# Four projection chunks of the HGRN2 mixer as two seven-product pairs, and re-spaced scans

## The chip, the core and the metric

The kernel runs on one NeuronCore of a Trainium2 chip. The metric is the device time of one execution in microseconds. PE is TensorE's matmul part, PEld its weight loads, DVE is VectorE, ACT ScalarE, POOL GpSimd and SP SyncE, which here only issues DMAs.

## The reference, cut to what matters

Two blocks of tokens (512 and 256, together T = 768, width D = 1024, float32) go through two layers. Each layer is half an FFN, a token mixer, and half an FFN; layer 0's mixer is a bidirectional gated linear recurrence (HGRN2), layer 1's is windowed attention. What matters here is the HGRN2 mixer:

```python
def hgrn2_mixer(x, w_in, w_o, g_norm, lb):
    """x: [B,T,D]; w_in: [D,5D] -> q | i | g | f_fwd | f_bwd; lb: [2, H*K] per-direction lower bounds."""
    q, i, g, f_fw, f_bw = jnp.split(x @ w_in, 5, axis=-1)
...
        f = lbd + (1.0 - lbd) * jax.nn.sigmoid(fpre.astype(F32))
        logf = jnp.log(f).reshape(B, T, H, K)
        k = (1.0 - f).reshape(B, T, H, K).astype(x.dtype)
...
    o_fwd = gla_chunk_scan(q, k_f, i, logf_f)
    o_bwd = rev(gla_chunk_scan(rev(q), rev(k_b), rev(i), rev(logf_b)))
    o = (o_fwd + o_bwd).astype(F32)
    o = o * lax.rsqrt(jnp.mean(o * o, axis=-1, keepdims=True) + NORM_EPS)
    o = o * g_norm.astype(F32).reshape(H, V)
    o = o.reshape(B, T, H * V).astype(x.dtype) * jax.nn.silu(g)
    return o @ w_o
```

`gla_chunk_scan` is the recurrence S_t = diag(f_t) S_{t-1} + k_t v_t^T, o_t = S_t^T q_t. There are 8 heads of 128 columns. Each head needs three chunks of the projection, 128 columns each: q (number 0), forward gate (3) and backward gate (4). Values (i) and output gate (g) are projected for all heads together.

## The kernel before, in words

**Float32 from three matmuls.** Each operand is split into a rounded high part (ACT, a cast) and a low remainder (DVE, a subtraction); a product is high x high + high x low + low x high, three matmuls (`mm3`, L312). Weights are loaded raw by SP into the pool "wr" (4 buffers), split into the pool "w" (8 buffers), and used. `plan` and `plan_quad` queue the weights, `ahead` and `take` stage as many as "w" holds, and `stage_next` (L272) loads further raw weights as buffers come free.

**Seven products for eight.** The FFN's up projections, the value, gate and output projections use a Strassen-like scheme: a 2 x 2 block product (two halves of the contraction by two halves of tokens or columns) is made from seven products in place of eight. The token side needs the blocks b00, b01, b10, b11 and the mixed factors t1 to t4, which `mix` (L420) and `put` (L410) make on DVE and ACT; each of the eight occupies two tiles of the pool "big" (21 buffers of 6 KB a partition). `up_pair` (L523) makes a gate and an up column block of the FFN so: seven `product` calls (L508) of 12 matmuls, 384 columns wide. The weight side of a pair (`quad_steps`, L181) takes two raw tiles, one more tile "s" of 256 KB, two accumulating DMAs on POOL's queue (`into`, L146), seven splits and two additions.

**The mixer's order.** `hgrn` (L971) traces, in this order:
1. the lead chunks, `LEAD` = q, forward and backward gate of head 0 and q of head 1, plainly by `hgrn_chunk` (L781): first all four for the first half of the tokens, then all four for the second. With the first half run the deferred steps of the FFN before (transposes, mixed factors, the spill of x);
2. the spill of the mixed factors (POOL's queue, `spill_factors`, L444);
3. the values, `tok_quad` (L742): seven products, 512 columns wide, order p1 p2 p7 p6 p5 p4 p3. Their raw weights (`tok_steps`, L228) take all four "wr" tiles, eight of eight scratch tiles "tA", two "s" and one "big". Inside them come the masks and head 0's gate arithmetic (`hgrn_gates`, L804);
4. one scan per head (`hgrn_scan`, L825). It has seven levels (L851 to L885). A level repacks the keys (L853, ACT), makes the scores of six blocks (L823, PE), evacuates them (`put`, L833: L837 or L842, DVE), multiplies the queries (L875), the keys (L879) and the totals (L881) on DVE. After the levels come transposes of the keys (L896), the states (L904, with a chain of ACT and DVE, L912 and L915) and the outputs (L928).

The scans' chains leave TensorE waiting, so `weave` (L711) puts filler between them: after each of the eight steps of a scan it takes pieces of a stream. The stream is the 20 plain chunks that remain (each six pieces of 9, 9 and 6 matmuls for either half) and then the gate projection (42 pieces). Before, a scan takes 16 pieces (head 0), 18 (heads 1 to 6) or 20 (head 7), evenly spread; what is left of the gate projection comes after.

The framework that builds the program orders each engine's instructions ahead of time, by when their inputs and buffers come free, so an instruction may stand far ahead of its place in the source.

Of the kernel before, what the change touches and what calls it, by code (L numbers as in the profile page):

```python
# [12 lines left out]
AF = mybir.ActivationFunctionType  # L13
# [20 lines left out]
SEQS = ((0, TA), (TA, TB))  # L34
H = T // 2
# [8 lines left out]
UP = ("p1", "p7", "p2", "p5", "p4", "p6", "p3")  # L44
TOK = ("p1", "p2", "p7", "p6", "p5", "p4", "p3")
TCHAIN = {"p2": "p1", "p4": "p5", "p3": "p7"}
OUT = ("p1", "p2", "p3", "p7", "p6", "p4", "p5")
LEAD = ((0, 0), (0, 3), (0, 4), (1, 0))
DOWN = ("p1", "p2", "p5", "p4", "p7", "p6", "p3")
FACTOR = {"p1": "b00", "p2": "b10", "p3": "b11", "p4": "t4", "p5": "t1", "p6": "t2", "p7": "t3"}  # L50


class Trunk:
# [356 lines left out]
    def put(self, name, kp, src, ops=None):  # L410
        if ops is None:
            ops = self.ops
        t = ops[(name, kp)] = self.big([P, 2, 2, H], F32R)
        self.split(src, t[:, :, 0, :], t[:, :, 1, :])
# [293 lines left out]
            yield  # L708

    @staticmethod  # L710
    def weave(main, feed, pieces, steps=LEVELS + 1, also=None):  # L711
        used = 0
        for i, _ in enumerate(main):
            if also:
                also(i)
            while used * steps < (i + 1) * pieces:
                used += 1
                next(feed, None)

    @staticmethod  # L720
# [21 lines left out]
    def tok_quad(self, key, order, chains, ops, evac, seed=None):  # L742
# [35 lines left out]
        for k in used:  # L778
            self.done(k)

    def hgrn_chunk(self, h, hd, c0, halves):  # L781
        key = ("hgrn", h, c0)
        wh, wl = self.take(key)
        if c0 == 0:
            if "qk" not in hd:
                hd["qk"] = self.big([P, 2, T])
            dst, func = hd["qk"][:, 0, :], AF.Copy
        else:
            if "f" not in hd:
                hd["f"] = self.big([P, 2, T])  # L790
            dst, func = hd["f"][:, 4 - c0, :], AF.Sigmoid
        for half in halves:
            ps = self.ps(H)
            for kk in range(NC):
                b = self.operand(f"b{kk // 4}{half}", kk % 4)
                self.mm3(ps, (wh[:, kk, :], wl[:, kk, :]), b, kk == 0, kk == NC - 1)
                if kk in (2, 5):
                    yield
            self.nc.scalar.activation(dst[:, half * H : (half + 1) * H], ps, func)
            if half:  # L800
                self.done(key)
            yield

    def hgrn_gates(self, h, hd):  # L804
        nc = self.nc
        qs, kd, f = hd["qk"][:, 0, :], hd["qk"][:, 1, :], hd["f"]
        q, k = (self.big([P, 2, T]) for _ in range(2))
        for d in range(2):
            fd, j = f[:, 1 - d, :], slice(h, h + 1)
            nc.vector.tensor_scalar(fd, fd, self.om_lb[:, d, j], self.lb[:, d, j], ALU.mult, ALU.add)  # L810
            nc.scalar.activation(k[:, d, :], fd, AF.Identity, bias=1.0, scale=-1.0)
            nc.vector.tensor_mul(q[:, 1 - d, :], qs, fd)
        nc.vector.tensor_add(kd, k[:, 0, :], k[:, 1, :])
        hd.update(h=h, qs=qs, kd=kd, q=q, k=k)

# [9 lines left out]
    def hgrn_scan(self, hd, v):  # L825
        nc = self.nc
        h, qs, kd, f, q, k = (hd[n] for n in ("h", "qs", "kd", "f", "q", "k"))
# [3 lines left out]
        blk = lambda t, b: t[:, b * P : (b + 1) * P]  # L831

        def put(level, pss):  # L833
            for s, (off, n) in enumerate(SEQS):
                dst = A[:, off : off + n]
                if level == 0:
                    nc.vector.tensor_copy(dst, pss[s])  # L837
                    continue
                nb = n // P
                m = self.masks[:, level, :].unsqueeze(1).to_broadcast([P, nb, P])  # L840
                r = lambda t: t.rearrange("p (b j) -> p b j", b=nb)
                nc.vector.copy_predicated(r(dst), m, r(pss[s]))  # L842
# [7 lines left out]
        tot, base = f, 0  # L850
        for l in range(LEVELS):  # L851
            c, J = T >> l, 1 << l
            nc.scalar.copy(packed(kop, J), picked(k, J))  # L853
# [12 lines left out]
            self.scan_scores(pss, lambda b: blk(kop, b), rhs)  # L866
            put(l, pss)
            if l == 0:
                pss = [self.ps(n) for _, n in SEQS]
                self.scan_scores(pss, lambda b: blk(kd, b), lambda b: blk(qs, b))  # L870
                put(LEVELS, pss)
            part = [list(q.ap[0])]
            both = bass.AP(q.tensor, q.offset, part + [[T + J, 2], [2 * J, c // 2], [1, J]])
            t = bass.AP(tot.tensor, tot.offset + base + 1, [list(tot.ap[0]), [T - 1, 2], [2, c // 2], [0, J]])
            nc.vector.tensor_mul(both, both, t)  # L875
            for d in range(2):
                xv = self.halves(k, l, d, d)
                t = tot[:, 1 - d, base + 1 - d : base + c : 2].unsqueeze(2).to_broadcast([P, c // 2, J])
                nc.vector.tensor_mul(xv, xv, t)  # L879
            nbase = 0 if l == 0 else base + c  # L880
            nc.vector.tensor_mul(  # L881
                totals[:, :, nbase : nbase + c // 2], tot[:, :, base : base + c : 2], tot[:, :, base + 1 : base + c : 2]
            )
            tot, base = totals, nbase
            yield  # L885

# [50 lines left out]
            )  # L937

    def plan_hgrn(self, w_in, w_o):
        def chunk(h, c):  # L940
            lo = c * D + h * P
            self.plan(("hgrn", h, c), w_in[:, lo : lo + P], (NC, P))

        for h, c in LEAD:
            chunk(h, c)
        def quad(key, w, order):
            rows = w.rearrange("(k m a p) c -> k m p a c", k=2, m=2, p=P)
            srcs = [[rows[k][m][:, :, c * 512 : (c + 1) * 512] for m in range(2)] for c in range(2) for k in range(2)]
            self.plan_quad(key, srcs, None, order)

        quad(("v",), w_in[:, D : 2 * D], TOK)
        for h in range(1, HEADS):
            for c in (0, 3, 4):
                if (h, c) not in LEAD:
                    chunk(h, c)
        quad(("g",), w_in[:, 2 * D : 3 * D], TOK)
        quad(("o",), w_o, OUT)

# [12 lines left out]
    def hgrn(self, lb_row, gn_row, next_row):  # L971
        nc = self.nc
# [5 lines left out]
        for half in range(2):  # L978
            for n, (h, c) in enumerate(LEAD):
                for i, _ in enumerate(self.hgrn_chunk(h, heads[h], c, (half,))):  # L980
                    if half == 0 and n and i != 1:
                        self.run_later()
            self.run_later(len(self.deferred))
        vs = {}

        def vtile(b):
# [22 lines left out]
        for at in self.tok_quad(("v",), TOK, TCHAIN, self.ops, evac_v):  # L1009
            if at == ("p6", HB - 1, 1):  # L1010
                self.load_masks()
                self.hgrn_gates(0, heads[0])
        scan = lambda hd: self.hgrn_scan(hd, vs)

        def stream():
            for h in range(1, HEADS):
                for c in (0, 3, 4):
                    if (h, c) not in LEAD:
                        yield from self.hgrn_chunk(h, heads[h], c, range(2))
                self.hgrn_gates(h, heads[h])  # L1020

        rs = self.cp.tile([P, HEADS, NBLK], F32, name="hrs")

# [78 lines left out]

        feed = itertools.chain(stream(), gate())
        for h in range(HEADS - 1):
            early = (lambda i, h=h: i in (1, 4) and len(ready) and scaled(*ready.pop(0))) if h > 3 else None
            self.weave(scan(heads[h]), feed, 16 if h == 0 else 18, also=early)
            if h == 3:
                rstds(0, 4)
                ready = [(i, i + 1) for i in range(4)]
        rstds(4, HEADS - 1)  # L1110
        self.weave(scan(heads[-1]), feed, 20, also=lambda i: i in (1, 3, 5) and scaled(4 + i // 2, 5 + i // 2))
        rstds(HEADS - 1, HEADS)
        scaled(HEADS - 1, HEADS)
        for i in range(HB):
# [445 lines left out]
```

## Time and profile before

| | us |
|---|---|
| median of 3 runs (2768.73 to 2769.39) | 2769.16 |
| the profiled execution | 2769.02 |
| its span, first to last instruction | 2767.2 |
| PE busy | 2745.0 (99%) |
| DVE busy | 2206.5 (80%) |
| lead chunks, second half | about 525.8 to 542.3 |
| values | 542.3 to 599.4 |
| scans of heads 0 to 7 | about 599.5 to 940 |

The profile's page gives busy time by engine, slices of the span, and the chain of work that ended last. Views of the trace give busy time in chosen stretches, groups of instructions by source line, a timeline, and waits with what ended them. Times within the span count from its first instruction. A row such as "L842 DVE ... x14 | 7.5, 585 | 2.4 <-PE ps L823 2.4" is line 842, on VectorE, 14 times, 7.5 us in all, 585 ns each, and 2.4 us of idle time before them that a matmul of line 823 ended.

### The profile page before, as it was taken

To read this page: it belongs to the slowest core of one execution; us is meant where nothing else is said; L and a number is where in the kernel's file an instruction comes from. 1 tells how busy PE (TensorE), PEld (TensorE's weight loads), DVE (VectorE), ACT (ScalarE), POOL (GpSimd) and SP (SyncE) were. 2 spreads that over 40 slices of the span, in tenths; PEclk is the share of its full clock that TensorE was granted. 3 is DMA by queue.
4 is the path that set the end of the run, shared out by engine and by line. 5 is a ranking of instruction groups with operands and counts; after the bars stand their busy time and mean duration, and the time that the engine had idled before them with its cause. 6 is when DMAs were issued, how large, how long until landed. Compare 5 with 4: busy or idle time off the path is not lost.

```text
span 2767.2 us, 40933 instructions
## 1 busy us (share of the span) xinstructions
PE 2745.0 (99%) x15117; PEld 2554.8 (92%) x15117; DVE 2206.5 (80%) x3766; ACT 1386.0 (50%) x2589; POOL 453.0 (16%) x491
## 2 busy tenths in 40 slices
PE   8999999999999999999999999999999999999998
PEld 8999999989999889999999999999888889999998
DVE  8788788767887888788878887887847868788877
ACT  7344444634455675444445543444458855444443
POOL 2111121200000101211111121111105611211111
PEclk9999999999999999999999999999999999999999
DMA  6554554851122743655444355544424422655443
GB/s 172 130 125 114 126 140 124 227 161 39 39 62 66 205 119 78 143 134 131 115 117 121 78 145 134 126 119 118 130 73 111 89 69 73 145 134 130 114 118 107
DMA packets 352040, 325.22 MB, mean 118 GB/s; under 512 B 14216, under 2 KB 271200, under 8 KB 351840
## 3 DMA queue, kind: packets, MB, share of 16 engines
q1 hardware_dynamic: 303040, 224.56, 27.7%
q0 software_dynamic: 44496, 84.56, 17.4%
q10 hardware_dynamic: 4304, 13.49, 1.3%
q8 instruction: 118, 1.93, 0.3%
q14 instruction: 82, 0.67, 0.1%
HBM read 225.82 MB, written 15.73 MB: 87 GB/s over the span
## 4 chain that ended last, share of the span: by engine, by line
PE 96%; DVE 2%; ACT 1%; DMA 1%; issue 0%; DVEq 0%; POOL 0%; SPq 0%; ACTq 0%; POOLq 0%
PE ps L513 42%; PE ps L577 21%; PE ps L315 6%; PE ps L316 6%; PE ps L314 6%; PE ps L760 5%; PE ps L823 3%; PE ps L928 1%; PE ps L1414 1%; PE ps L904 1%; PE ps L385 1%; PE ps L1426 0%; PE ps L1376 0%; PE ps L1427 0%; PE ps L1377 0%; PE ps L1181 0%
## 5 line engine op out<-in xcount | busy, mean ns | idle before, releaser
L513 PE MATMUL ps<-big,w 128*128 128x384 f32 x6720 | 1169.3, 334 | 0.0
L513 PEld LDWEIGHTS ps<-big,w 128*128 128x128 f32 x6720 | 1165.9, 188 | 1.7 <-ACT tA L530 0.2
L208 ACT CAST w<-wr 128x512 fp32r<-128x512 f32 x600 | 415.8, 707 | 689.2 <-PE ps L513 274.9
L577 PE MATMUL ps<-w,big 128*128 128x512 f32 x2520 | 575.7, 390 | 0.0
L577 PEld LDWEIGHTS ps<-w,big 128*128 128x128 f32 x2520 | 472.7, 188 | 98.0 <-ACT big L319 0.4
L209 DVE TENSOR_TENSOR w<-wr,w 128x512 fp32r<-128x512 f32 (+1 forms) x520 | 438.0, 846 | 145.9 <-ACT w L208 123.9
L147 POOL DMA_DIRECT2D s<-wr x126 | 109.8, 878 | 1250.3 <-DMA s<-in_ffn_w_dram 432.0
L599 DVE SCALAR_TENSOR_TENSOR x<-ps,x 128x512 f32<-128x512 f32 x468 | 302.4, 686 | 10.1 <-PE ps L316 10.0
L314 PE MATMUL ps<-big,w 128*128 128x384 f32 x640 | 219.6, 345 | 1.2 <-ACT w L175 0.9
L315 PE MATMUL ps<-big,w 128*128 128x384 f32 x640 | 215.7, 337 | 0.7 <-DVE big L320 0.7
L316 PE MATMUL ps<-big,w 128*128 128x384 f32 x640 | 214.6, 335 | 0.0
L319 ACT CAST big<-tA 128x384 fp32r<-128x384 f32 x296 | 148.0, 513 | 115.4 <-DVE tA L545 37.0
L147 POOL DMA_DIRECT2D wr<-wr x109 | 94.9, 871 | 518.3 <-DMA wr<-in_ffn_w_dram 165.9
L760 PE MATMUL ps<-w,big 128*128 128x512 f32 x756 | 177.1, 392 | 0.1
L320 DVE TENSOR_TENSOR big<-tA,big 128x384 fp32r<-128x384 f32 x296 | 168.0, 578 | 6.7 <-ACT big L319 4.7
L209 POOL TENSOR_TENSOR w<-wr,w 128x512 fp32r<-128x512 f32 x80 | 137.4, 1718 | 197.8 <-ACT w L208 195.8
L760 PEld LDWEIGHTS ps<-w,big 128*128 128x128 f32 x756 | 140.6, 188 | 29.1 <-DVE w L320 0.6
L215 DVE TENSOR_TENSOR wr<-wr,wr 128x512 f32<-128x512 f32 (+1 forms) x120 | 123.3, 1027 | 25.9 <-issue 23.6
L314 PE MATMUL ps<-w,big 128*128 128x512 f32 x336 | 134.6, 401 | 0.1
L316 PE MATMUL ps<-w,big 128*128 128x512 f32 x336 | 131.8, 392 | 0.5 <-DVE big L400 0.5
L315 PE MATMUL ps<-w,big 128*128 128x512 f32 x336 | 131.8, 392 | 0.0
L315 PEld LDWEIGHTS ps<-big,w 128*128 128x128 f32 x640 | 120.6, 188 | 2.0 <-DVE big L320 1.7
(214 smaller groups left out, 3504.0 us busy)
## 6 DMA issues: line engine op xcount, KB each, us to landing
wr<-in_ffn_w_dram SPq DMA_DIRECT2D x264, 512.0 KB, 4.0
s<-wr POOLq DMA_DIRECT2D x126, 256.0 KB, 4.8
s<-in_ffn_w_dram SPq DMA_DIRECT2D x120, 256.0 KB, 3.2
wr<-wr POOLq DMA_DIRECT2D x80, 256.0 KB, 3.8
wr<-in_hg_w_in_dram SPq DMA_DIRECT2D x32, 512.0 KB, 3.9
wr<-wr POOLq DMA_DIRECT2D x29, 512.0 KB, 4.6
spill<-x ACTq DMA_DIRECT2D x12, 512.0 KB, 4.0
kept<-big POOLq DMA_DIRECT2D x8, 768.0 KB, 9.7
```

The lines of the kernel that those rows point to most:

```text
L147: self.nc.gpsimd.dma_start(out, src, accum_op=ALU.add)
L208: nc.scalar.copy(h, src)
L209: (eng or nc.vector).tensor_sub(l, src, h.bitcast(F32))
L314: nc.tensor.matmul(out, a[0], b[0], start=first, stop=False)
L315: nc.tensor.matmul(out, a[0], b[1], start=False, stop=False)
L316: nc.tensor.matmul(out, a[1], b[0], start=False, stop=last)
L319: self.nc.scalar.copy(hi, src)
L320: self.nc.vector.tensor_sub(lo, src, hi.bitcast(F32))
L513: self.nc.tensor.matmul(ps, a[x], b[y], start=first and k == 0 and i == 0, stop=k == 3 and i == 2, skip_group_check=True,)
L577: nc.tensor.matmul(ps, a[x], w[y], start=name == chain and kp == 0 and q == 0, stop=kp == 1 and q == 2, skip_group_check=True,)
L599: self.nc.vector.scalar_tensor_tensor(x, ps, c, x, ALU.mult, ALU.add)
L760: nc.tensor.matmul(ps, x[:, sl], y, start=fresh and k == 0 and q == 0, stop=k == 3 and q == 2, skip_group_check=True,)
```

## The change

- Four chunks, (1,3), (1,4), (2,0) and (2,3) (head, number), leave the filler stream. They become two pairs, made by seven products each between the lead chunks and the values. `hgrn_pair` is `up_pair` with other ends: the results go to the heads' tiles, through a sigmoid for gates.
- The weights of the two pairs are planned as `UP` quads between the lead chunks and the values.
- The scans take fewer pieces, from a table by step: 14 for heads 0 to 5, 16 for head 6, 20 for head 7. The stream runs further ahead of the scans, and a head's gate arithmetic is done in steps 5, 6 and 7 of the scan before it.
- In a scan's level, keys, totals and queries are multiplied before the scores are evacuated.

```diff
+PAIRS = (((1, 3), (1, 4)), ((2, 0), (2, 3)))
+PIECES = ((2, 2, 2, 2, 2, 2, 1, 1), (2, 2, 2, 2, 2, 2, 2, 2), (3, 3, 3, 2, 3, 2, 2, 2))
...
-    def weave(main, feed, pieces, steps=LEVELS + 1, also=None):
-        used = 0
+    def weave(main, feed, pieces, also=None):
         for i, _ in enumerate(main):
             if also:
                 also(i)
-            while used * steps < (i + 1) * pieces:
-                used += 1
+            for _ in range(pieces[i]):
                 next(feed, None)
...
+    def hgrn_pairs(self, heads):
+        def args(one, two):
+            return ("hgrn", one), self.hgrn_dst(heads[one[0]], one[1]), self.hgrn_dst(heads[two[0]], two[1]), self.tmp(H), self.tmp(H)
+
+        return [self.hgrn_pair(*a) for a in [args(*pair) for pair in PAIRS]]
+
+    def hgrn_pair(self, key, one, two, v, w):
...
+        p("p1", a, True, False)
+        nc.scalar.copy(v, a)
+        self.ahead()
+        p("p7", c, True, False)
+        nc.scalar.copy(w, c)
+        self.ahead()
+        p("p2", a, False, True)
+        nc.scalar.activation(x0, a, fx)
+        self.ahead()
+        p("p5", d, True, False)
+        nc.vector.tensor_sub(w, w, d)
+        self.ahead()
+        p("p4", c, False, True)
+        p("p6", b, True, True)
+        nc.vector.tensor_sub(v, v, b)
+        nc.vector.tensor_sub(y0, c, v)
+        end(y0, fy)
+        nc.vector.tensor_sub(y1, w, v)
+        end(y1, fy)
+        self.ahead()
+        p("p3", d, False, True)
+        nc.vector.tensor_add(x1, v, d)
+        end(x1, fx)
+        self.ahead()
+        yield
...
             nc.vector.tensor_mul(q[:, 1 - d, :], qs, fd)
+            yield
         nc.vector.tensor_add(kd, k[:, 0, :], k[:, 1, :])
...
             self.scan_scores(pss, lambda b: blk(kop, b), rhs)
-            put(l, pss)
-            if l == 0:
-                pss = [self.ps(n) for _, n in SEQS]
-                self.scan_scores(pss, lambda b: blk(kd, b), lambda b: blk(qs, b))
-                put(LEVELS, pss)
-            part = [list(q.ap[0])]
-            both = bass.AP(q.tensor, q.offset, part + [[T + J, 2], [2 * J, c // 2], [1, J]])
-            t = bass.AP(tot.tensor, tot.offset + base + 1, [list(tot.ap[0]), [T - 1, 2], [2, c // 2], [0, J]])
-            nc.vector.tensor_mul(both, both, t)
             for d in range(2):
                 xv = self.halves(k, l, d, d)
...
             nc.vector.tensor_mul(
                 totals[:, :, nbase : nbase + c // 2], tot[:, :, base : base + c : 2], tot[:, :, base + 1 : base + c : 2]
             )
+            part = [list(q.ap[0])]
+            both = bass.AP(q.tensor, q.offset, part + [[T + J, 2], [2 * J, c // 2], [1, J]])
+            t = bass.AP(tot.tensor, tot.offset + base + 1, [list(tot.ap[0]), [T - 1, 2], [2, c // 2], [0, J]])
+            nc.vector.tensor_mul(both, both, t)
+            put(l, pss)
+            if l == 0:
+                pss = [self.ps(n) for _, n in SEQS]
+                self.scan_scores(pss, lambda b: blk(kd, b), lambda b: blk(qs, b))
+                put(LEVELS, pss)
...
         for h, c in LEAD:
-            chunk(h, c)
+            self.plan(("hgrn", h, c), cols(h, c), (NC, P))
+        for one, two in PAIRS:
+            self.plan_quad(("hgrn", one), (cols(*one), cols(*two)), (NC, P), UP)
...
             self.run_later(len(self.deferred))
+        self.drain(itertools.chain(*self.hgrn_pairs(heads)))
         vs = {}
...
         for h in range(HEADS - 1):
-            early = (lambda i, h=h: i in (1, 4) and len(ready) and scaled(*ready.pop(0))) if h > 3 else None
-            self.weave(scan(heads[h]), feed, 16 if h == 0 else 18, also=early)
+            gates = []
+
+            def also(i):
+                if h > 3 and i in (1, 4) and ready:
+                    scaled(*ready.pop(0))
+                if h + 1 in made:
+                    if not gates:
+                        gates.append(self.hgrn_gates(h + 1, heads[h + 1]))
+                    if i in (5, 6, 7):
+                        next(gates[0], None)
+
+            self.weave(scan(heads[h]), feed, PIECES[h > 5], also=also)
+            self.drain(gates[0] if gates else self.hgrn_gates(h + 1, heads[h + 1]))
...
-        self.weave(scan(heads[-1]), feed, 20, also=lambda i: i in (1, 3, 5) and scaled(4 + i // 2, 5 + i // 2))
+        self.weave(scan(heads[-1]), feed, PIECES[2], also=lambda i: i in (1, 3, 5) and scaled(4 + i // 2, 5 + i // 2))
```

More of the change, by code (lines that the diff above doesn't have):

```diff
@@ L779, in tok_quad, with hgrn_dst, end @@
             self.done(k)
+    def hgrn_dst(self, hd, c0):
+        name, at = ("f", 4 - c0) if c0 else ("qk", 0)
+        if name not in hd:
+            hd[name] = self.big([P, 2, T])
+        return hd[name][:, at, :], AF.Sigmoid if c0 else AF.Copy
+    def hgrn_pairs(self, heads):
[3 more added lines that the diff above has]
+    def hgrn_pair(self, key, one, two, v, w):
+        nc = self.nc
+        a, b, c, d = (self.ps(H) for _ in range(4))
+        p = lambda name, ps, first, last: self.product(key, name, FACTOR[name], ps, first, last)
+        (x, fx), (y, fy) = one, two
+        x0, x1, y0, y1 = x[:, :H], x[:, H:], y[:, :H], y[:, H:]
+        def end(t, func):
+            if func != AF.Copy:
+                nc.scalar.activation(t, t, func)
+        p("p1", a, True, False)
[23 more added lines that the diff above has]
+        yield
     def hgrn_chunk(self, h, hd, c0, halves):
@@ L783, in hgrn_chunk @@
         wh, wl = self.take(key)
[L784 to L791, printed above, removed]
+        dst, func = self.hgrn_dst(hd, c0)
         for half in halves:
@@ L939, in plan_hgrn, with cols @@
     def plan_hgrn(self, w_in, w_o):
-        def chunk(h, c):
+        def cols(h, c):
             lo = c * D + h * P
-            self.plan(("hgrn", h, c), w_in[:, lo : lo + P], (NC, P))
+            return w_in[:, lo : lo + P]
         for h, c in LEAD:
-            chunk(h, c)
+            self.plan(("hgrn", h, c), cols(h, c), (NC, P))
+        for one, two in PAIRS:
+            self.plan_quad(("hgrn", one), (cols(*one), cols(*two)), (NC, P), UP)
         def quad(key, w, order):
@@ L951, in plan_hgrn @@
         quad(("v",), w_in[:, D : 2 * D], TOK)
[L952 to L955, printed above, removed]
+        self.rest = [(h, c) for h in range(1, HEADS) for c in (0, 3, 4) if (h, c) not in (*LEAD, *itertools.chain(*PAIRS))]
+        for h, c in self.rest:
+            self.plan(("hgrn", h, c), cols(h, c), (NC, P))
         quad(("g",), w_in[:, 2 * D : 3 * D], TOK)
@@ L1011, in hgrn @@
                 self.load_masks()
-                self.hgrn_gates(0, heads[0])
+                self.drain(self.hgrn_gates(0, heads[0]))
         scan = lambda hd: self.hgrn_scan(hd, vs)
+        made = {h for h in range(1, HEADS) if h not in [i for i, _ in self.rest]}
         def stream():
[L1016 to L1020, printed above, removed]
+            left = list(self.rest)
+            while left:
+                h, c = left.pop(0)
+                yield from self.hgrn_chunk(h, heads[h], c, range(2))
+                if h not in [i for i, _ in left]:
+                    made.add(h)
         rs = self.cp.tile([P, HEADS, NBLK], F32, name="hrs")
```

## The prediction

> **What bounds the kernel now.** I read the page first: the busy shares, the slices and the chain that ended last.
>
> ```profile
> span 2767.2 us, 40933 instructions
> PE 2745.0 (99%) x15117; PEld 2554.8 (92%) x15117; DVE 2206.5 (80%) x3766; ACT 1386.0 (50%) x2589; POOL 453.0 (16%) x491
> PEclk9999999999999999999999999999999999999999
> PE 96%; DVE 2%; ACT 1%; DMA 1%; issue 0%; DVEq 0%; POOL 0%; SPq 0%; ACTq 0%; POOLq 0%
> ```
>
> TensorE is busy 99% of the span, at full clock, and it is 96% of the chain. A busy matmul row need not mean full pace, so the second view is the busy time in stretches: the second half of the lead chunks, the value projection, and one whole scan period (from one head's first scores to the next head's). The third view lists what TensorE waited for between 500 and 1000 us.
>
> ```profile
> 517.50:542.30 24.80, 24.80 (x144) 24.80 (x144) 20.33 (x24) 17.29 (x27) 6.06 (x8) 1.00 0.54 163
> 542.40:599.40 57.00, 57.00 (x253) 47.19 (x252) 32.83 (x45) 22.91 (x33) 7.29 (x10) 1.00 0.75 215
> 680.87:722.71 41.84, 41.84 (x294) 41.54 (x293) 33.51 (x59) 18.25 (x35) 0.00 (x0) 1.00 0.14 39
> PE ps L928 <- DVE big L915: 0.4, 1, 0.4
> PE ps L315 <- DVE big L320: 0.3, 1, 0.3
> PE ps L904 <- ACT big L897: 0.2, 1, 0.2
> ```
>
> The columns of the first three rows are the stretch, its length, then busy time and count of PE, weight loads, DVE, ACT and POOL, then clock, DMA share and GB/s. TensorE is without a gap in all three, and its waits in 500 us come to 0.9 us. So **the mixer costs what its matmuls cost**: fewer matmuls help at once, and no moved wait can give more than 0.9 us here. A 384-wide matmul takes 24.80/144 = 0.172 us, a 512-wide one of the values 57.00/252 = 0.226 us.
>
> **What it removes and adds on TensorE.** A plain chunk is 2 halves x 8 x 3 = 48 matmuls; four are 192. A pair is 7 products x 12 = 84; two are 168. That is 24 fewer of the same width: 192 x 0.172 = 33.07 us go, 168 x 0.172 = 28.93 us come, **-4.13 us**. All else on TensorE only moves: 24 filler pieces (8 matmuls each on average) leave the scans and the pairs stand ahead of the values.
>
> [...]
>
> **The scans with less filler.** A steady period loses 4 of 18 pieces, 4 x 8 x 0.172 = 5.51 us, and becomes 36.33 us. DVE, 33.51 us now, loses only the splitting of two thirds of a chunk (1.22 us by the L176 row below): 32.7 us, 90% of the new period. So DVE doesn't become the bound on average; what matters is the order inside a period.
>
> ```profile
> 645.43 1.23 DVE L176 TENSOR_TENSOR w<-wr,w 128x1024 fp32r<-128x1024 f32 x1 [1.88 <-ACT w L175]
> 651.05 1.07 DVE L842 COPY_PREDICATED big<-masks,ps 128x512 f32<-128x512 uint8 x2 [0.38 <-PE ps L823]
> 652.01 0.93 DVE L875 TENSOR_TENSOR big<-big,big 128x768 f32<-128x768 f32 x1
> 652.98 0.36 DVE L881 TENSOR_TENSOR big<-big 128x192 f32<-128x192 f32 x1
> 653.44 1.03 DVE L879 TENSOR_TENSOR big<-big,big 128x384 f32<-128x384 f32 x2
> 651.54 0.84 ACT L853 COPY big<-big 128x768 f32<-128x768 f32 x1 [0.89 <-PE ps L823]
> ```
>
> Within a level the next scores need the repacked keys (L853, 0.84 us behind the last scores) and the multiplied queries (L875). Today L875 stands behind the evacuation L842, so the chain from the last scores is about 0.5 + 0.93 us (651.5 to 652.94), and two pieces (2.75 us) cover it. The new order puts the evacuation last, which shortens the chain to about 1 us, so levels with two pieces stay covered. I cost the reorder at **nothing**: DVE does the same instructions. If that cover failed, a level would lose at most 1.4 us, its chain without filler.
>
> The end of a scan is tighter. There transposes (L896), the copies of them, the state products (L904), the DVE chain L915 and the output products (L928) follow one another:
>
> ```profile
> 672.26 1.03 PE L896 MATMUL ps<-ident_r,big 128*128 128x128 f32 x8
> 673.05 0.42 PE L314 MATMUL ps<-big,w 128*128 128x384 f32 x1
> 673.95 2.05 PE L904 MATMUL ps<-x,big 128*128 128x128 f32 x16
> 675.75 0.42 PE L315 MATMUL ps<-big,w 128*128 128x384 f32 x1
> 676.33 0.73 DVE L915 SCALAR_TENSOR_TENSOR big<-big,big,ps 128x128 f32<-128x128 f32 x2 [0.16 <-ACT big L912]
> 677.75 0.27 PE L928 MATMUL ps<-x,big 128*128 128x128 f32 x1
> ```
>
> Filler covers 673.05 to 673.95 and 675.75 to 677.75. Needed are the first 0.90 us and, up to the end of L915 at 677.06, 1.31 us: 2.21 us. Two pieces remain behind the last level instead of four or more; the first goes ahead of the transposes, the second (9 or 6 matmuls) gives 1.55 or 1.03 us. The shortfall is 0.66 to 1.18 us a scan, unless filler of the next scan's first step or its first scores come forward. Bounds for seven scans: 0 and 7 x 1.18 = 8.3 us. I take 1.0 us, near the lower end, because the nearest row, the 0.9 us of all waits, shows such gaps filled in every scan so far.
>
> The gate arithmetic of the next head (L810 to L813, five DVE and two ACT instructions, the same as now) goes to steps 5 to 7, beside that L915 chain; I put its cost into the same 0 to 8.3 us. So too with the chunks that now run a head further ahead and hold one to two more tiles at the seam between scans: the next scan's packed operands then wait for the transposed keys, but they are needed only behind L928.
>
> **The pairs and the values behind them.** A pair's seven 512-wide splits cost ACT 7 x 0.707 us and DVE six of 0.846 us, two adds of 1.027 us, and one split on POOL of 1.718 us; its evacuation five DVE instructions of 0.55 us:
>
> ```profile
> L208 ACT CAST w<-wr 128x512 fp32r<-128x512 f32 x600 | 415.8, 707 | 689.2 <-PE ps L513 274.9
> L209 DVE TENSOR_TENSOR w<-wr,w 128x512 fp32r<-128x512 f32 (+1 forms) x520 | 438.0, 846 | 145.9 <-ACT w L208 123.9
> L209 POOL TENSOR_TENSOR w<-wr,w 128x512 fp32r<-128x512 f32 x80 | 137.4, 1718 | 197.8 <-ACT w L208 195.8
> L215 DVE TENSOR_TENSOR wr<-wr,wr 128x512 f32<-128x512 f32 (+1 forms) x120 | 123.3, 1027 | 25.9 <-issue 23.6
> L544 DVE TENSOR_TENSOR tA<-ps,tA 128x384 f32<-128x384 f32 x2 | 1.1, 554 | 0.0
> L513 PE MATMUL ps<-big,w 128*128 128x384 f32 x6720 | 1169.3, 334 | 0.0
> ```
>
> That is 9.9 us of DVE in 14.5 us of products; the FFN runs the same pattern 6720/84 = 80 times, and its matmuls (L513, last row) show 0.0 us of idle time before them. Cost: **nothing**; without that cover, the second product would wait for the mixed factor t3.
>
> The pools are the new thing. The pool "big" has 21 buffers. During the values 16 hold operands (8 of the blocks, 8 of the mixed factors), three hold the lead chunks and one the values' own extra raw tile: 20. The pairs write three more tiles, which makes 23. That buffers are handed out in program order, even while some are free, shows here:
>
> ```profile
> 530.81 0.48 ACT L799 ACTIVATE big<-ps 128x384 f32<-128x384 f32 x1
> 534.18 0.49 ACT L799 ACTIVATE big<-ps 128x384 f32<-128x384 f32 x1
> 540.60 0.47 ACT L799 ACTIVATE big<-ps 128x384 f32<-128x384 f32 x1
> 542.26 0.87 ACT L799 ACTIVATE big<-ps 128x384 f32<-128x384 f32 x2
> 552.86 0.85 ACT L811 ACTIVATE big<-big 128x768 f32<-128x768 f32 x1 [0.76 <-DVE w L320]
> 566.40 1.20 ACT L853 COPY big<-big 128x768 f32<-128x768 f32 x1
> ```
>
> The second half of the four lead chunks is 96 matmuls, 16.5 us before 542.3, so the first half was multiplied by 525.8. Yet five evacuations (L799) come after that where the second half has four: chunk (1,0) waited for its buffer, behind the mixed factors that come before it in the program. L811 began when L320 released the raw tile, and the scan's first L853 only when the third value product had released t3. So the second pair's evacuations must wait about until then too, its two scratch tiles (of 8 "tA") with them, and the values' raw loads need all eight of those. The loads also lose their lead: now they are issued from 484 on, 58 us ahead; then only as the pairs' weights are split, some 15 to 20 us ahead.
>
> ```profile
> 484.30 1.89 SPq L237 DMA_DIRECT2D tA<-in_hg_w_in_dram  x4
> tA<-in_hg_w_in_dram SPq DMA_DIRECT2D x16, 256.0 KB, 4.4
> tA<-tA POOLq DMA_DIRECT2D x8, 256.0 KB, 5.3
> kept<-big POOLq DMA_DIRECT2D x8, 768.0 KB, 9.7
> 540.00:560.00 20.00, 20.00 (x93) 16.95 (x92) 11.70 (x16) 12.84 (x22) 6.68 (x10) 1.00 1.05 309
> ```
>
> SP's queue gets six loads of the pairs ahead of the values' (four of them stood in the scans), and POOL's gets four accumulating DMAs ahead of the eight spills, in a stretch where the DMA engines are full (share 1.05). ACT copies of the second pair's scratch would hold back ACT's evacuations behind them. Cost: at the lower bound nothing, because the first three value products (3 x 36 x 0.226 = 24.4 us) need none of the late tiles; at the upper bound the chain of a load (4.4), two accumulates (5.3 each) and two last splits (2 x 0.85 by the L209 row) = 16.7 us. I take 0.6 us, near the lower end: the list of waits above holds none of this kind, and the products that come first cover more than the chain.
>
> **Sum.** The profiled execution took 2769.02 us (span 2767.2 and 1.8 around it), 0.14 below the median of three, 2769.16. 2769.02 - 4.13 + 1.0 + 0.6 = **2766.5 us**. What this kernel's measurement can tell from no change is about 0.2%, 5.5 us, so this counts as no difference.
>
> **Rivals.** *Buffer wait in the values (slower).* It decides if the pair's scratch is served ahead of the raw loads, so that the last raw tile loads only after the third product. TensorE could then still run halves of the next products: 18 matmuls, then 12 as PSUM's eight banks allow, 6.8 us. 16.7 - 6.8 = 9.9 us: 2766.5 - 0.6 + 9.9 = 2775.8, to 2782.6 with no cover. For it: 23 tiles for 21 buffers, full DMA. Against: loads that come first in program order get scratch first. [...]
>
> *Uncovered scan ends.* 8.3 us in place of 1.0: 2773.8. For it: the shortfall above, and DVE at 90%. Against: filler from ahead.
>
> The next rival rests on when DVE writes the last mixed factor now:
>
> ```profile
> 542.73 0.95 DVE L320 TENSOR_TENSOR big<-big,big 128x768 fp32r<-128x768 f32 x1
> ```
>
> *It doesn't gain what it says.* The first pair's second product needs t3 at about 544.4, and DVE writes the last mixed factors until 543.7 with a fuller queue than now; if pairs start 2 to 4 us late, the gain is gone: 2769.
>
> *Faster by over 0.2%.* It would need 1.4 us beyond the count of matmuls, where the mixer's waits hold 0.9.
>
> **How the numbers follow.** Forecast (2764.5 to 2768.5) 0.50; uncovered scan ends 0.15; no gain 0.12; buffer wait 0.19; faster 0.04. Faster by over 0.2% is 0.04, within 0.2% 0.50 + 0.15 + 0.12 = 0.77, slower 0.19. The range runs from 2763.5 (leaving out the 0.04) to 2777, which takes in the middle of the buffer wait and leaves about 0.12 of it out.
>
> **What would show it.** Right: 168 L513-like matmuls at 0.172 us between lead and values, no wait of PE above 1 us there; scan periods of about 36.3 us, with DVE at 90%; L842 behind L875. Wrong: idle time at L760 released by ACT or DVE splits (the buffers or the loads), L928 waiting for L915 in each scan (the cover), or the second product waiting for a big tile (the mix).

## The result: slower by 0.15%

The changed kernel takes 2772.93 us (median of 22 runs, 2771.38 to 2774.55), beside 2768.89 for the kernel before (22 runs): a ratio of 1.0015, 95% interval 1.0008 to 1.0021. The forecast was 2766.5 us, 2.5 less than the profiled execution of before. The profiled execution spans 2771.2 us, 4.0 more than before. Line numbers below are those of the changed kernel or of the experiment named: L515 is a product of a pair (L513 before), L760 the values, L866 the scores, L896 and L899 the packing of keys and queries (L853 and L856 before), L947 the states, L955 and L958 their chain on ACT and DVE (L912 and L915 before), L971 the outputs.

First the page's lines that answer to those of before, of the changed kernel:

```profile
span 2771.2 us, 40955 instructions
PE 2744.3 (99%) x15093; PEld 2552.6 (92%) x15093; DVE 2207.9 (80%) x3788; ACT 1391.9 (50%) x2602; POOL 465.8 (17%) x497
PE 93%; ACT 2%; DMA 2%; DVE 2%; issue 1%; POOL 0%; SPq 0%; DVEq 0%; ACTq 0%; POOLq 0%
L515 PE MATMUL ps<-big,w 128*128 128x384 f32 x6888 | 1200.4, 334 | 3.1 <-ACT tA L805 3.1
```

The 24 matmuls are gone (15117 to 15093). TensorE's share of the chain fell from 96 to 93%, and the products, which had no idle time before them, have 3.1 us. What TensorE waited for from 500 to 1040 us:

```profile
PE ps L515 <- ACT tA L805: 3.1, 1, 3.1
PE ps L866 <- ACT big L899: 1.0, 2, 0.5
PE ps L947 <- ACT big L940: 0.7, 3, 0.2
PE ps L317 <- DVE big L322: 0.7, 2, 0.4
PE ps L971 <- DVE big L958: 0.4, 1, 0.4
```

One wait is large and stands alone; the others are the scans' (L866, L947, L971) and two that before has too (L317, and one of 0.2 us at L316 that is not shown). The stretches around the large one (columns as in the prediction):

```profile
541.80:564.69 22.89, 22.89 (x134) 22.89 (x133) 15.79 (x23) 9.83 (x18) 7.68 (x9) 1.00 0.88 324
564.69:591.20 26.51, 26.43 (x116) 21.32 (x115) 9.06 (x13) 11.10 (x17) 10.35 (x12) 1.00 1.03 244
594.20:598.00 3.80, 3.77 (x13) 3.78 (x14) 1.17 (x3) 0.54 (x2) 0.00 (x0) 0.59 0.61 155
```

TensorE makes the first pair and four products of the second (to 564.69), goes on with 115 matmuls of the values, stands still from about 591, and makes the second pair's last three products at 594, at a granted clock of 0.59 at first. The timeline says the same in one row, ACT's rows beside it what it waited for, and POOL's row which transfer that was:

```profile
594.23 8.08 PE L515 MATMUL ps<-big,w 128*128 128x384 f32 x36 [3.11 <-ACT tA L805]
```

```profile
589.80 0.62 ACT L321 CAST w<-tA 128x512 fp32r<-128x512 f32 x1 [0.60 <-DMA tA<-tA]
590.33 1.04 ACT L321 CAST w<-wr 128x1024 fp32r<-128x1024 f32 x1
593.69 0.48 ACT L805 COPY tA<-ps 128x384 f32<-128x384 f32 x1 [2.32 <-DMA tA<-tA]
```

```profile
589.12 0.86 POOL L149 DMA_DIRECT2D tA<-tA  x1 [0.88 <-DMA tA<-tA]
```

The copy at 593.69 is the second pair's first write into its scratch tile, 29 us after its first four products were done (564.69). It waited for an accumulating DMA between two raw tiles of the values, behind the split of such a tile (L321, w<-tA). By the source (`tok_steps`) it is the raw tile from which the fourth value product, p6, is split and which is then added to that of p2. The 36 matmuls took 7.91 us from the first one's start to the start of the next value matmul at 602.14 (the row's 8.08 takes in the end of the last, which overlaps with that one), where 36 x 0.172 = 6.19 are due: **3.1 us of wait and 1.7 of slow clock**. With 0.2 more in the step that holds the wait, and 0.2 spread over the other steps from 541.8 to 602.1, it is 5.2 together. (The expectations below give the slow clock as 1.9; their sum of 5.2 is the same.)

The scans lose the rest. I counted the steps from one matmul's start to the next that exceed the matmul's own pitch (the median step of its width) by over 0.14 us, and summed what they exceed it by, between 600 and 960 us: 1.4 us before, 4.6 after. Losses in the scans are counted so from here on; waits are those of the trace. So -4.1 + 5.2 + 3.2 = +4.3 us, where the spans differ by 4.0.

### The profile page after: what moved, and what is told of

The parts are those of the page before. It is cut to its first block, busy times and chain, and to the rows that moved or that the text cites. A ratio compares the mean times of both kernels' runs of the same rounds, so it can differ in the third digit from the quotient of the medians.

```text
span 2771.2 us, 40955 instructions
## 1 busy us (share of the span) xinstructions
PE 2744.3 (99%) x15093; PEld 2552.6 (92%) x15093; DVE 2207.9 (80%) x3788; ACT 1391.9 (50%) x2602; POOL 465.8 (17%) x497
## 4 chain that ended last, share of the span: by engine, by line
PE 93%; ACT 2%; DMA 2%; DVE 2%; issue 1%; POOL 0%; SPq 0%; DVEq 0%; ACTq 0%; POOLq 0%
PE ps L515 42%; PE ps L579 21%; PE ps L317 6%; PE ps L316 6%; PE ps L318 6%; PE ps L760 4%; PE ps L866 3%; PE ps L971 1%; PE ps L1474 1%; DMA tA<-tA 1%; PE ps L387 1%; DMA tA<-in_hg_w_in_dram 0%; PE ps L1436 0%; PE ps L1437 0%; PE ps L1486 0%
## 5 line engine op out<-in xcount | busy, mean ns | idle before, releaser
L515 PE MATMUL ps<-big,w 128*128 128x384 f32 x6888 | 1200.4, 334 | 3.1 <-ACT tA L805 3.1
L515 PEld LDWEIGHTS ps<-big,w 128*128 128x128 f32 x6888 | 1196.6, 188 | 5.2 <-ACT tA L805 3.5
L210 ACT CAST w<-wr 128x512 fp32r<-128x512 f32 x612 | 423.1, 705 | 691.0 <-PE ps L515 278.5
L321 ACT CAST big<-tA 128x384 fp32r<-128x384 f32 x296 | 148.0, 513 | 114.8 <-DVE tA L547 36.9
L316 PE MATMUL ps<-big,w 128*128 128x384 f32 x576 | 198.1, 346 | 0.9 <-ACT w L177 0.7
L317 PE MATMUL ps<-big,w 128*128 128x384 f32 x576 | 193.7, 336 | 0.8 <-DVE big L322 0.7
L318 PE MATMUL ps<-big,w 128*128 128x384 f32 x576 | 193.4, 336 | 0.0
L211 POOL TENSOR_TENSOR w<-wr,w 128x512 fp32r<-128x512 f32 x82 | 145.2, 1771 | 196.2 <-ACT w L210 196.1
L760 PE MATMUL ps<-w,big 128*128 128x512 f32 x756 | 177.4, 392 | 0.1
L760 PEld LDWEIGHTS ps<-w,big 128*128 128x128 f32 x756 | 140.5, 188 | 29.4 <-DVE w L322 0.8
L316 PE MATMUL ps<-w,big 128*128 128x512 f32 x336 | 134.5, 400 | 0.1
L317 PE MATMUL ps<-w,big 128*128 128x512 f32 x336 | 131.8, 392 | 0.0
L317 PEld LDWEIGHTS ps<-big,w 128*128 128x128 f32 x576 | 108.5, 188 | 2.0 <-DVE big L322 1.8
```

The costliest lines, as they stand in the source:

```text
L210: nc.scalar.copy(h, src)
L211: (eng or nc.vector).tensor_sub(l, src, h.bitcast(F32))
L316: nc.tensor.matmul(out, a[0], b[0], start=first, stop=False)
L317: nc.tensor.matmul(out, a[0], b[1], start=False, stop=False)
L318: nc.tensor.matmul(out, a[1], b[0], start=False, stop=last)
L321: self.nc.scalar.copy(hi, src)
```

## The experiments

**Theory A**: the second pair's scratch stands in the queue of the pool tA behind the values' eight raw tiles. **Rival B**: the values' loads are late because the DMA engines are full, whatever the scratch lies in. For the scans, **S1**: too little filler. Another theory, **S3**, came out of the traces and is stated below.

### Both pairs' scratch elsewhere

```diff
-            return ("hgrn", one), ..., self.tmp(H), self.tmp(H)
+            spare = heads[one[0] - 1]["qk"][:, 1, :]
+            return ("hgrn", one), *dsts, spare[:, :H], spare[:, H:]
```

> The scratch of both pairs lies in the idle halves of two query tiles instead of two tA tiles each; nothing else changes. Theory A (the second pair's scratch stands in the tA pool's queue behind the eight raw tiles of the values, and gets a tile only when the fourth value product has been split): the 3.1 us wait at 594 us and the 1.9 us of half clock behind it go, since all eight tA tiles serve the values and can be loaded during the lead chunks; both pairs run in one piece before the first value product; 2772.9 - 5.2 = 2767.7 us, values' end near 628 us. Rival B (the raw loads and accumulating DMAs of the values are late because the DMA engines are full while the pairs run, whatever the scratch lies in): the wait stays within 1 us of 3.1 and moves to a value product (L760); 2771.5 to 2773.5 us. Both: scan periods as in the changed kernel, 36.2 to 39 us.

2768.83 us, ratio 0.9999 (0.9990 to 1.0008): 4.1 less than the changed kernel and 1.1 above A's figure, within the interval of 2.5 us to either side; the span is 2766.4. Its pairs and values, and SP's first loads:

```profile
541.63:570.90 29.27, 29.27 (x170) 29.27 (x170) 18.11 (x26) 12.85 (x23) 11.21 (x13) 1.00 0.89 299
570.75:627.90 57.15, 57.15 (x253) 47.29 (x253) 33.20 (x47) 22.50 (x33) 8.03 (x9) 1.00 0.68 165
```

```profile
483.60 2.00 SPq L239 DMA_DIRECT2D tA<-in_hg_w_in_dram  x4
```

Both stretches are without a gap and at full clock, and the values' raw tiles are loaded from 484 on (the other four from 488), as before the change. In the changed kernel they start at 545 (below). That fits A, but here the loads are early as well, so B is not out yet.

### The second pair's scratch alone

The same edit for the second pair only; the first keeps its tA tiles.

> Only the second pair's scratch lies in the idle half of a query tile; the first pair keeps its two tA tiles, so that two of the eight raw tiles of the values still come free only inside the first pair, as in the changed kernel. Theory A: the second pair no longer waits; 36 matmuls less stand between the third and the fourth value product, the raw loads are as late as in the changed kernel, and at most 1 us of wait is left at L760 for the fourth product; 2767.7 to 2768.7 us. Rival B: TensorE comes to the fourth value product before its splits (they ended near 594 us in the changed kernel) and waits 2 to 4 us there, with the half clock behind it: 2771.5 to 2773.5 us.

2768.49 us, 0.9998 (0.9990 to 1.0007), within A's range. The loads now are as late as in the changed kernel. SP there, and then SP in this one:

```profile
545.29 7.70 SPq L239 DMA_DIRECT2D tA<-in_hg_w_in_dram  x6
...
565.63 1.41 SPq L239 DMA_DIRECT2D tA<-in_hg_w_in_dram  x2
```

```profile
546.04 8.16 SPq L239 DMA_DIRECT2D tA<-in_hg_w_in_dram  x6
...
566.16 0.98 SPq L239 DMA_DIRECT2D tA<-in_hg_w_in_dram  x2
```

```profile
542.55:571.83 29.28, 29.28 (x170) 29.28 (x170) 18.12 (x26) 12.85 (x23) 9.51 (x12) 1.00 0.92 338
```

Loads at the same times, DMA as full (share 0.92, beside 0.88 in the changed kernel), and no wait: the pairs run in one piece, and TensorE waits nowhere in the values. **B falls, A stands**: late loads alone cost nothing here; the second pair's place in the queue for scratch costs the wait and the slow clock behind it. Whether two more tiles in tA, or its tiles taken ahead of the loads, would do the same was not run.

### Plain chunks at the pairs' place

```diff
-        self.drain(itertools.chain(*self.hgrn_pairs(heads)))
+        for h, c in itertools.chain(*PAIRS):
+            self.drain(self.hgrn_chunk(h, heads[h], c, range(2)))
```

> The four chunks stand at the same place, ahead of the values, but are made as plain chunks of 48 matmuls each, 192 in place of the pairs' 168; no scratch, scans as in the changed kernel. It tells what the pairs save and what the scans alone cost. Theory A: 24 x 0.172 = 4.1 us more of matmuls, no wait for tA and no half clock, 5.2 us less: 2771.8 us, PE without a wait over 1 us between 540 and 640 us. Theory S (the scans lose 3.3 us to thin ends, whatever stands ahead of the values): 2768.9 + 3.3 = 2772.2 us, scan ends with the same waits as in the changed kernel. Rival B: the same crowding, 3 to 5 us of waits at L760: 2775 to 2777 us.

2771.80 us, 1.0013 (1.0004 to 1.0022): as A and S both said. There is no wait in the values. The 192 plain matmuls:

```profile
542.36:575.43 33.07, 33.07 (x193) 33.07 (x191) 7.82 (x10) 6.25 (x10) 8.43 (x11) 1.00 0.94 264
```

33.07 us against about 29.1 for both pairs (541.63 to 570.75 above): the pairs give 3.9 of the 4.1 us that were counted. And the re-spaced scans cost 2.9 us by themselves: this kernel has the same matmuls as before, and 4.6 us of loss in the scans, at the same places as the changed kernel.

### The new order in a level, alone

The kernel before, with keys, totals and queries multiplied ahead of the evacuation.

> The kernel before with the new order inside a level alone (keys, totals and queries multiplied ahead of the evacuation of the scores). The prediction's step (the reorder costs nothing): 2768.9 us within 0.6, no new wait above 0.3 us in a scan. Rival R (the evacuation behind three multiplications holds the score banks, and the S chain at a scan's end comes later): 0.3 to 0.5 us in each of eight scans, 2771 to 2773 us, so that part of the changed kernel's loss in the scans is the order's and not the missing filler's.

2768.85 us, 1.0001 (0.9992 to 1.0010), 0.95 us of loss in its scans: the order costs nothing, as forecast.

### The old order, with thin scans

The moved scratch, and the evacuation ahead of the multiplications again.

> The version with both pairs' scratch in idle halves and the old order inside a level (evacuation of the scores first, then queries, keys, totals): it tells what the new order is worth once the scans have only 14 pieces. The prediction's step (levels with two pieces are covered in either order, a level without cover loses at most 1.4 us): 2768.8 to 2770.2 us. Rival O (the old chain of scores, evacuation, queries, next scores is not covered by two pieces at DVE 90% busy): 0.5 us or more on each of six levels in seven scans, 2780 us or above.

2779.94 us, 1.0039 (1.0026 to 1.0051), 11.1 above the same kernel with the new order; its scans lose 14.3 us, not 4.6. Its largest wait and three single ones:

```profile
PE ps L870 <- ACT big L900: 7.6, 6, 2.1
```

```profile
656.14 0.38 PE L870 MATMUL ps<-big,big 128*128 128x128 f32 x1 [2.07 <-ACT big L900]
724.58 0.38 PE L870 MATMUL ps<-big,big 128*128 128x128 f32 x1 [2.07 <-ACT big L900]
805.75 0.51 PE L870 MATMUL ps<-big,big 128*128 128x128 f32 x2 [2.07 <-ACT big L900]
```

Scores wait for packed keys (L900 here). These come later because the keys are multiplied behind the evacuation and the queries; it is the late levels, where the next head's gates also stand on DVE. But that is only part of it, as DVE's row for the keys and ACT's rows ahead of the third wait show:

```profile
802.49 1.02 DVE L926 TENSOR_TENSOR big<-big,big 128x384 f32<-128x384 f32 x2
```

```profile
803.54 1.04 ACT L177 CAST w<-wr 128x1024 fp32r<-128x1024 f32 x1 [3.08 <-PE ps L317]
804.50 0.48 ACT L845 ACTIVATE big<-ps 128x384 f32<-128x384 f32 x1
804.88 0.82 ACT L900 COPY big<-big 128x768 f32<-128x768 f32 x1
```

The keys were ready at 803.51, but ACT split a weight (L177) and evacuated a chunk (L845) first and packed them from 804.88 on. The other two waits have the same rows, so 1.2 to 1.4 of each 2.07 us lie in the order on ACT; no run here fixes that order to test it. The time lies just under the rival's bound, but in a few levels and not in each, as the rival had it. So the reorder, worth nothing in the kernel before, is worth 11.1 us with scans of 14 pieces.

### The scans' ends: filler or order?

A seam is where one head's scan ends and the next one's begins. In the changed kernel's seams ACT's rows show something that before has at one seam alone:

```profile
738.51 0.27 ACT L955 COPY big<-ps 128x128 f32<-128x128 f32 x1 [0.76 <-PE ps L947]
738.67 1.19 ACT L896 COPY big<-big 128x768 f32<-128x768 f32 x1
739.75 1.19 ACT L899 COPY big<-big 128x768 f32<-128x768 f32 x1
740.84 0.44 ACT L955 COPY big<-ps 128x128 f32<-128x128 f32 x2
```

The next scan's packing (L896, L899) stands between the first state copy and the second. At all seven seams its keys, at five of them its queries too, go ahead of the last two copies. **S3**: the next head's gates are ready so early that its packing goes ahead of the state copies and holds up the chain to the outputs. In the kernel before, the packing (L853) comes behind three of the four copies (L912) at the first six seams:

```profile
675.14 0.27 ACT L912 COPY big<-ps 128x128 f32<-128x128 f32 x1 [0.76 <-PE ps L904]
676.03 0.43 ACT L912 COPY big<-ps 128x128 f32<-128x128 f32 x2 [0.63 <-PE ps L904]
...
676.77 1.18 ACT L853 COPY big<-big 128x768 f32<-128x768 f32 x1
```

At the seventh it came behind the first copy before the change too (884.52), and there lies the one wait for the state chain that before has, the 0.4 us at L928 in the prediction's list. The remedy fixes ACT's order:

```diff
+            with self.tc.issue_after(self.last_s) if l == 0 and self.last_s else nullcontext():
-            nc.scalar.copy(packed(kop, J), picked(k, J))
+                nc.scalar.copy(packed(kop, J), picked(k, J))
...
-                    nc.scalar.copy(S[:, i, :], ds)
+                    self.last_s = nc.scalar.copy(S[:, i, :], ds).ins
```

> The version with both pairs' scratch in idle halves; besides, ACT packs the next scan's first keys and queries (two copies of 1.19 us) only behind the four state copies of the scan that ends, by a fixed order on ACT. In the changed kernel one or both of them stand between the first and the last of those four copies. Theory S3 (the next head's gates are ready so early now that its packing goes ahead of the state copies and holds up the state chain): the waits for the state chain (0.2 to 0.6 us, four of them) and for the query packing (0.24 to 0.66, three) go or shrink; the loss in the scans falls from 4.6 to about 2 us; 2766.3 us. Theory S1 (two pieces of filler are too few beside the tail, whatever the order on ACT): the loss stays within 0.7 us of 4.6; 2768.8 us.

2766.54 us, 0.9990 (0.9982 to 0.9999), forecast 2766.3. The same seam, and TensorE's waits:

```profile
732.61 0.27 ACT L961 COPY big<-ps 128x128 f32<-128x128 f32 x1 [0.76 <-PE ps L953]
733.50 0.43 ACT L961 COPY big<-ps 128x128 f32<-128x128 f32 x2 [0.63 <-PE ps L953]
734.02 1.05 ACT L177 CAST w<-wr 128x1024 fp32r<-128x1024 f32 x1
734.98 0.26 ACT L961 COPY big<-ps 128x128 f32<-128x128 f32 x1
735.13 0.49 ACT L846 ACTIVATE big<-ps 128x384 f32<-128x384 f32 x1
735.51 1.19 ACT L902 COPY big<-big 128x768 f32<-128x768 f32 x1
```

```profile
PE ps L953 <- ACT big L946: 0.7, 3, 0.2
PE ps L871 <- ACT big L905: 0.7, 2, 0.4
```

The outputs wait for no state chain any more, and the scans lose 2.9 us, not 4.6. Two runs for S1:

> The version with both pairs' scratch in idle halves, and in the first six scans one piece of filler moved from behind the first level to behind the states (1 2 2 2 2 2 1 2 in place of 2 2 2 2 2 2 1 1): as many pieces in a scan, another place. Theory S1: 1.03 to 1.55 us more cover for the state chain, the waits of the output products and of the next scores (2.9 us of the 4.6) go; 2766.0 us, unless the first level then lacks its cover (a new wait of 0.3 to 1 us each). Theory S3: the packing would be hoisted as before, the state chain stays late; within 0.7 us of 2768.8.

2767.78 us, 0.9996 (0.9987 to 1.0006): between the two theories. The outputs' waits for the state chain went from four to two, but two of 1.0 us for the transposed keys (L944 here) came; 4.3 us of loss. So filler at the end has a price where it was taken, and S1 is not refuted by this run.

> The version with both pairs' scratch in idle halves, and in the first six scans a second piece behind the states, taken from the last two scans (16 to 14 and 20 to 16 pieces), so that the total stays 120. Theory S1: the six scans lose 2.9 us less, scan seven loses some 0.7 us more as its filler is now that of the others: 2766.6 us. Theory S3: 2768.8 us within 0.7, as the order on ACT stays.

2768.85 us, 1.0000 (0.9991 to 1.0009): no gain from 1.38 us more filler in each of six scans, though it was taken from the last two. Most of the short waits are gone, but one of 2.15 us for the query packing (L903) stands at the first seam, where ACT packs the queries only behind the evacuation of the outputs, and two of 0.4 us in the last scan; 4.8 us of loss. So the order on ACT, fixed without any more filler, gave more than filler that was moved: S3 stands for 1.7 of the 3.2 us. Is it separate from the wait for tA, and what is the rest?

> The changed kernel with its scratch where it was (tA), and only the fixed order on ACT added (the next scan's first packing behind the four state copies). Are the two causes separate? If they are: the 3.1 us wait for tA and the half clock behind it stay, the scans' loss falls from 4.6 to 2.9 us as it did beside the moved scratch: 2772.9 - 2.3 = 2770.6 us. If the scans' loss hangs on when the values end: another time, 2768 or 2773 us.

2770.83 us, 1.0009 (1.0000 to 1.0018); the 3.1 us wait for tA stands, and the scans lose 2.9 us: the two causes add up.

> Moved scratch and fixed order on ACT; besides, in the first six scans one piece moves from behind the first level to behind the last (1 2 2 2 2 2 2 1). Left of the waits are the transposed keys' copies (0.4 us, two in these scans) and the next scores' packing (0.48 and 0.56). Theory S1 for this rest (too little filler ahead of the transposes' copies): the two 0.4 us waits go, 2765.7 us. Against: the piece is missed at the first level, which then waits up to 0.5 us in each of six scans: 2767 to 2769 us.

2766.19 us, 0.9992 (0.9983 to 1.0000). The waits and the periods are those of the fixed order alone, to 0.05 us: this piece's place in the table decided nothing, and neither forecast came true.

> Moved scratch and fixed order on ACT; besides, in the first six scans one piece moves from behind the first level to behind the states (1 2 2 2 2 2 1 2). Without the fixed order this move gave 1.05 us and two waits of 1.11 us for the transposed keys. If the fixed order has already taken what filler behind the states can give (S3): 2766.5 to 2768.5 us, the 1.11 us waits are there. If both add up (S1 beside S3): 2765.5 us.

2765.92 us, 0.9990 (0.9982 to 0.9999), the lowest of all, 7.0 us under the changed kernel; but its loss in the scans (3.05 us, with two waits of 1.0 for the transposed keys, as S3 had it) is as large as with the fixed order alone, and 0.6 us of median can't be told from it. The time lies between the two forecasts.

> Moved scratch and fixed order on ACT; besides, the next head's gates (five DVE and two ACT instructions) are issued from the third level on, as soon as their chunks are made, and not beside the last two levels and the states. If the gates' DVE time (about 5 us) at the end of a scan is what the rest of the waits (0.4 to 0.56 us, four in the first six scans) comes from: these go, 2765.0 us. If not: 2766.5 us within 0.6; above it if the gates now delay a level's multiplications.

2766.78 us, 0.9993 (0.9984 to 1.0002), with the same waits, to 0.01 us: the gates' place isn't their cause. Some 1.5 us of the scans' 3.2 stay with no single cause shown.

## Why the prediction was wrong, step by step

- **-4.13 us of matmuls: right.** 33.07 became about 29.1, at 0.173 us each.
- **The pairs' splits and t3 in time: right.** The pairs run without a gap where their scratch is there (29.27 us); "no gain" was not the case.
- **The reorder costs nothing: right** (1.0001). But "if that cover failed, a level would lose at most 1.4 us" was too small for what the old order would have lost: 2.07 us of wait at each of three levels.
- **Values and buffers, "I take 0.6 us": the step that failed.** Measured 5.2, within its bounds of 0 and 16.7; this alone turns the 2.5 us of gain into a loss. The text had the parts: buffers granted in program order, eight tA tiles that the values need all, a second pair held back. It then looked only for what the *values* would wait for, and judged that "loads that come first in program order get scratch first" speaks against the rival. The statement was true, and it was the mechanism: the loads took the tiles, and the second pair's scratch, first written behind them, had to wait until the raw tile of the fourth value product had been split and added to another. The rival's "decides if the pair's scratch is served ahead of the raw loads" had the sign reversed; its wait came at a product of the second pair and not at the values (L760), and to 3.1 us and not to 9.9, as TensorE had 115 value matmuls to do first (26.4 us, 564.69 to 591.12).
- **The clock behind the wait.** The forecast has no term for it. Behind the wait of 3.11 us the granted clock was 0.50 for 3.41 us, and the 36 matmuls took 1.7 us more than the 6.19 that were due.
- **Scan ends, "I take 1.0 us": the second term that was too small.** Measured 3.2, within 0 to 8.3. The shortfall of filler was counted with the state chain's length of before; but the chain itself grew, as one or two copies of 1.19 us from the next scan went into it (1.7 of the 3.2 us; the rest has no single cause shown). That the next scan's packed operands "are needed only behind L928" overlooked that they could also come too early. And "such gaps filled in every scan so far" was not so: 0.4 of the 0.9 us in that list is L928's wait for the chain.
- **"About 0.2%, 5.5 us": too coarse.** With 22 runs of each kernel the interval is 0.13% wide, and 4.0 us are clear of no change.
- **DVE at 90% of a period: near.** 31.12 of 36.43 us, 85%, in the second scan:

```profile
670.55:706.98 36.43, 36.08 (x260) 35.62 (x259) 31.12 (x58) 16.86 (x32) 0.00 (x0) 1.00 0.10 30
```

With 5.2 and 3.2 in place of 0.6 and 1.0 the sum gives 2769.02 - 4.13 + 3.2 + 5.2 = 2773.3, beside the measured 2772.93. Two of the rivals (the buffer wait, 2775.8, and the uncovered scan ends, 2773.8) were each about half of what happened, together and not one in place of the other; that the time fell near the second one's figure is chance.

## What to carry to other kernels

When work is put ahead of a stage that shares a scratch pool with it, write down the order in which every user is served, and ask for each one, the new work too, which earlier user must give its tile back and when. Work that becomes ready earlier is not free either: on an engine that serves a chain it can go in front of that chain, as one or two copies of 1.19 us did on ACT here, so a list of "what is late next" needs its twin, "what is early now". And a change that measures as nothing alone (the order in a level) can be what another part of the same change rests on: 11.1 us here.

## What the runs showed of the hardware

In the changed kernel a granted clock of 0.50 stands behind the wait of 3.11 us (591.12 to 594.23), for one stretch of 3.41 us:

```profile
591.47:594.88 3.41, 0.66 (x4) 0.66 (x5) 0.83 (x2) 0.48 (x1) 0.00 (x0) 1.00 1.04 163
594.88:598.29 3.41, 3.41 (x12) 3.41 (x11) 0.90 (x2) 0.83 (x2) 0.00 (x0) 0.50 0.51 151
598.29:601.70 3.41, 3.41 (x21) 3.41 (x21) 1.90 (x3) 2.11 (x5) 0.00 (x0) 1.00 0.32 91
```

The stretch at 0.50 holds 12 matmuls where the next one, at 1.00, holds 21. Of the three waits of 2.07 us in the kernel with the old order, the first (to 656.14) and the second (to 724.58) have a granted clock of 1.00 behind them, the third (to 805.75) one of 0.55:

```profile
656.14:659.54 3.40, 3.40 (x25) 3.36 (x26) 3.02 (x7) 0.00 (x0) 0.00 (x0) 1.00 0.52 154
724.58:727.98 3.40, 3.40 (x24) 3.40 (x25) 3.40 (x7) 0.84 (x1) 0.00 (x0) 1.00 0.53 154
...
805.75:809.15 3.40, 3.40 (x15) 3.40 (x16) 2.48 (x6) 0.68 (x1) 0.00 (x0) 0.55 0.53 154
```

The last stretch holds 15 matmuls where the first two hold 25 and 24. From 809.80 to 811.50 the granted clock is 1.00 again. So in this kernel the length of a wait did not decide alone: behind 2.07 us the clock stayed full twice and fell once. What decides was not shown.
